# 128-row gathers and scatters in a new order of slots, a third matmul round in a branch of TensorE, and a 21st weight buffer

## The chip, the core and the metric

The kernel runs on one core of a Trainium2 chip. The metric is the device time of one execution in microseconds; a kernel's time is the median of its runs. The profile names the engines PE (TensorE, matmuls), PEld (its weight loads), DVE (VectorE), ACT (ScalarE), POOL (GpSimd) and SP (SyncE, which issues most DMAs); a "q" behind a name is the engine's sequencer or queue. The core's DMAs run on 16 DMA engines.

## What is computed

One decoder layer for 512 prompt tokens and 32 sample tokens (8 sequences of 4): a gated short convolution and a forgetting attention, merged by gates and projected, layer norm, and then a mixture of 16 experts, again with layer norm. The change lies in the experts:

```python
def hier_moe(x, w_group, w_router, w1, w3, w2):
    t = x.reshape(N * S, D)                       # 544 tokens (prompt and sample), D = 1024
    gp = jax.nn.softmax(t @ w_group)              # 4 groups, the best one is taken
    p_g, g_idx = lax.top_k(gp, 1)
    el_sel = ...                                  # the 4 experts of that group
    top_w, top_i = lax.top_k(jax.nn.softmax(el_sel), 2)
    gate = ...                                    # 544 x 16, two entries a row
    for e in range(16):
        h = jax.nn.silu(t @ w1[e]) * (t @ w3[e])  # 1024 -> 512
        y = y + gate[:, e:e + 1] * (h @ w2[e])    # 512 -> 1024
```

Each token goes to two of 16 experts, 68 tokens to an expert in the mean. All weights are float32; those of one expert are 6 MB.

## The kernel before

Up to about 447 us the kernel does the projections, the convolution, the attention, the output projection, the first layer norm and the routing. Then come the experts, which need 96 pieces of weights of 1 MB, and from about 720 us on the last sums and the second layer norm.

**Slots.** For each expert the tokens that chose it get positions 1, 2, 3 and so on (`pos`). `slot` (L370) holds the numbers 1 to `CAP` = 96. `onehots` compares both, `place` and `place_early` turn the result by a small matmul into 96 row numbers (`gix`), and `gate_of` puts the gates beside them. A slot without a token gets a row number past the end, and the DMA leaves such rows out. A branch at the end of the program (L1505) covers experts with over 96 tokens; with these inputs there are none.

**Gather and scatter.** `gather` (L1117) is an indexed DMA that POOL issues: it fetches the tokens' rows of 4 KB from `x1d` in DRAM into one of `NXG` = 3 buffers `xg`, a partition a slot. At the end of `down` (L1277) a second one adds the rows of `y` (one of `YB` = 2 buffers) to `acc` in DRAM. The last two experts (`KC` = 2) are not scattered but kept (`down_kept`) and summed on PE at the end.

**Matmuls of an expert.** `x_t` transposes the gathered rows. `up` multiplies in three rounds g = 0, 1, 2 of 32 slots each: the 32 slots are the stationary operand, and four matmuls, one for each quarter of the output columns, fill the array's four column strips. For each of 8 k-slices all three rounds run one after another. `glu` applies silu and the product, `h_t` transposes, and `down` works in rounds too: two for the first 64 slots, a third for slots 65 to 96. ACT scales `py` by the gates into `y`.

**The weights.** `raw_load` takes the buffers of a ring `RING` of 20 in turn and lets SP issue the load (L798). Pieces 13 and 14 wait for the last row of the first layer norm, pieces 17 to 21 (`GATED`) for the landing of the first gather, and from the 21st on each waits for the landing of the piece five before it (`AHEAD`, L800). A piece also waits until its buffer's last reader is done. The order is: the up pieces of expert e (four), then the down pieces of expert e-1 (two); at the end up pieces 0 and 1 of expert 15, the down pieces of 14, the rest of 15.

**The order in the loop** over experts, body e: first half of `up(e)`; transposes of x for e+1; second half of `up(e)`; `place` and `gather` for expert e+1+`NXG`; `down(e-1)`; `glu(e)`. Each engine runs its instructions in order; the framework adds the semaphores.

Of the kernel before, what the change touches and what calls it, by code (L numbers as in the profile page):

```python
# [55 lines left out]
WB = 4  # L56
KC = 2
ORDER = (4, 0, 1, 2, 3)
RING = ["pre"] * NPRE + ["rawb"] * NRB + ["raw"] * 2 + ["whl"] * 4 + ["half"] * 6
LAG = 2  # L60
MID = 4
FIRST = (1, 2, 3, 0, 4)
# [13 lines left out]
ZPE = (3, 4)  # L76
AHEAD = 5
THR0 = 20
YB = 2
NXG = 3  # L80
VW = 260
HELD = (13, 14)
GATED = (17, 18, 19, 20, 21)
# [4 lines left out]
def layer_kernel(ctx: ExitStack, tc: tile.TileContext, i_, o_):  # L88
# [238 lines left out]
    with tc.issue_after(ln_done.ins):  # L327
# [39 lines left out]
    nc.gpsimd.iota(prow, pattern=[[0, 1]], base=0, channel_multiplier=1)  # L367
    pcol = const.tile([128, 1], F32, name="pcol")
    nc.vector.tensor_copy(pcol, prow)
    slot = const.tile([128, CAP], BF, name="slot")  # L370
    nc.gpsimd.iota(slot, pattern=[[1, CAP]], base=1, channel_multiplier=0,
                   allow_small_or_imprecise_dtypes=True)
    rn = pa.tile([128, 2], F32, name="rn")
    rni = pa.tile([128, 2], I32, name="rni")
    nc.vector.tensor_single_scalar(rni[:, 0:1], prow, 5, op=ALU.arith_shift_right)
# [401 lines left out]
    def raw_load(e, j):  # L777
        shape, srcs = piece_of(e, j)
        shape = [128] + shape
        name = "wd" if j > 3 else "we"  # L780
        kind = ring_order[ring["n"] % len(ring_order)]
        ring["n"] += 1
        if kind == "half":
            r = half(name, shape)
        elif kind == "pre":
            r = pr_p.tile(shape, F32, name=name, tag="pre", bufs=NPRE)
        elif kind == "raw":
            r = base_p.tile(shape, F32, name=name, tag="raw", bufs=2)
        elif kind == "whl":
            r = base_p.tile(shape, F32, name=name, tag="whl", bufs=WB)  # L790
        else:
            r = p2.tile(shape, F32, name=name, tag="rawb", bufs=NRB)
        with ExitStack() as st:
            if ring["n"] in HELD:
                st.enter_context(tc.issue_after(last_x1.ins))
            elif ring["n"] > NPRE:
                st.enter_context(tc.issue_after(x_load.ins))
            lds = [nc.sync.dma_start(r if i is None else r[:, i], s) for s, i in srcs]  # L798
# [72 lines left out]
    xgs = []  # L871
    for b in range(NXG):
        xgs.append(p2.tile([128, D], F32, name=f"xg{b}"))
    nc.gpsimd.memset(xgs[0], 0.0)
    rsm = xgs[0]
    res = [rbig[t // 2][:, t % 2] for t in range(4)] + [rsm]
# [11 lines left out]
    for a in range(2):  # L888
        nc.gpsimd.tensor_mul(wr3[:, a, :, :NR], wrr,
                             gb[:, a].unsqueeze(2).to_broadcast([128, 8, NR]))  # L890
    ln_g, ln_b = lnw(1, xgs[1:])

    def small(name, shape, dt=F32):
        return p2.tile([128] + shape, dt, name=name)
# [45 lines left out]

    sums_last = []
    zt_last = {}
    wk = []

    def parts_of(x, n, cm=None):
        t = order[x]
# [2 lines left out]
        for k in range(4):  # L949
            nc.tensor.transpose(pp[:, k, :m], res[t][:m, (4 * n + k) * 128:(4 * n + k + 1) * 128], ident[:m, :m])  # L950
        if (x, n) == (NT - 1, 1):
            wk.append(ps_mm("wake")[:, 0])
# [34 lines left out]
    def ln1_out(x):  # L987
        t = order[x]
        m = rows_of(t)
        sc = mvs[:m, t]  # L990
        x1 = p2.tile([128, D], F32, name="x1", tag="y", bufs=YB) if x < NT - 1 else rsm
        if x < NT - 1:
            nc.scalar.activation(x1[:m], res[t][:m], AF.Identity, bias=sc[:, 4:5], scale=sc[:, 3:4])
            nc.vector.tensor_mul(x1[:m], x1[:m], ln_g[:m])
# [79 lines left out]
    flat = "p t e -> p (t e)"  # L1074
    asf = asb.rearrange("p t g e -> p t (g e)")
    mm(pps[:, :NT * NE], before, asf.rearrange(flat), start=False, stop=True, skip_group_check=True)
    keep_warm(wk[0], WK[3])
    pos = small("pos", [NT, NE], BF)
    nc.vector.scalar_tensor_tensor(pos.rearrange(flat), pps[:, :NT * NE], 1.0, asf.rearrange(flat),
# [7 lines left out]
    onehot = {}  # L1087

    def onehots(e):
        oh = p2.tile([128, NT, CAP], BF, name="soh", tag="soh", bufs=2)  # L1090
        nc.vector.tensor_tensor(oh, slot.unsqueeze(1).to_broadcast([128, NT, CAP]), bc(pos[:, :, e], CAP),
                                op=ALU.is_equal)
        onehot[e] = oh
        return oh

    def gate_of(e, parts):
        nc.vector.tensor_reduce(gat[:CAP, e:e + 1], parts, axis=AX, op=ALU.add)
        if e < E0:
            nc.scalar.activation(gat2[64:, e, 0:1], gat[:64, e:e + 1], AF.Copy)
            for q in range(4):  # L1100
                nc.scalar.activation(gat2[32 * q:32 * q + 32, e, 1:2], gat[64:96, e:e + 1], AF.Copy)

    def to_index(e, me):
        return nc.vector.tensor_scalar(gix[:CAP, e:e + 1], me, FAR, None, op0=ALU.add)  # L1104

    def place(e):
        pmt = ps_s("pmt")
        oh = onehots(e)
        for x in range(NT):
            mm(pmt[:CAP, :5], oh[:, x], mv[:, x, e], start=x == 0, stop=x == NT - 1)  # L1110
        me = p2.tile([CAP, 1], F32, name="me", tag="me", bufs=2)
        nc.vector.tensor_reduce(me, pmt[:CAP, 0:2], axis=AX, op=ALU.add)
        to_index(e, me)
        gate_of(e, pmt[:CAP, 2:5])

    def gather(e):
        return nc.gpsimd.indirect_dma_start(out=xgs[e % NXG][:CAP], out_offset=None, in_=x1d,  # L1117
                                     in_offset=bass.IndirectOffsetOnAxis(ap=gix[:CAP, e:e + 1], axis=0),
                                     bounds_check=T - 1, oob_is_err=False)

    def place_early(e):
        oh = onehots(e)
        pm0 = ps_s("pm0")
        for x in range(NT):
            mm(pm0[:CAP, :1], oh[:, x], tokh[:, x:x + 1], start=x == 0, stop=x == NT - 1)
        return to_index(e, pm0[:CAP, :1]), gather(e)

    def gates_early(e):
        oh = onehot[e]
        pg0 = ps_s("pg0")  # L1130
        for x in range(NT):
            mm(pg0[:CAP, :3], oh[:, x], mv[:, x, e, 2:5], start=x == 0, stop=x == NT - 1)
# [8 lines left out]
    oh1 = small("oh1", [NT, NE])  # L1141
    oh2 = small("oh2", [NT, NE])
# [54 lines left out]

    def rows_by_two(xr):  # L1200
        return xr.rearrange("c (j p r) -> c j r p", p=128, r=2)

# [21 lines left out]
    def up_round(g, pab, x, raws, ks):  # L1224
        out = pab.rearrange("p a b -> p (a b)")[:, 256 * g:256 * g + 256].rearrange("p (a b f) -> p a b f", a=2, f=32)
        for k in ks:
            rhs = raws[k // 2][:, :, k % 2].rearrange("p a (b c f) -> p a b c f", c=4, f=32)
            for c in range(4):
                mm(out[32 * c:32 * c + 32], x[:, k, 32 * g:32 * g + 32], rhs[:, :, :, c], start=k == 0 and g != 1,  # L1229
                   stop=k == 7, skip_group_check=True)  # L1230
# [25 lines left out]
    def down_round(r, py, h, raws, ks):  # L1256
        for k in ks:
            for q in range(4):
                g, c = (q % 2, 2 * (q // 2) + r) if r < 2 else (2, q)
                mm(py[32 * q:32 * q + 32, 256 * r:256 * r + 256], h[:, k, 32 * g:32 * g + 32],  # L1260
                   raws[k // 2][:, k % 2, 256 * c:256 * c + 256], start=k == 0 and r != 1, stop=k == 3,
                   skip_group_check=True)

    def down(e, h):
# [7 lines left out]
        nc.scalar.activation(y[:64, :512], py[:64, :512], AF.Copy, scale=gat[:64, e:e + 1])  # L1272
        nc.scalar.activation(y[:64, 512:], py[64:, :512], AF.Copy, scale=gat2[64:, e, 0:1])
        for q in range(4):
            nc.scalar.activation(y[64:, 256 * q:256 * q + 256], py[32 * q:32 * q + 32, 512:768], AF.Copy,  # L1275
                                 scale=gat2[32 * q:32 * q + 32, e, 1:2])
        nc.gpsimd.indirect_dma_start(out=acc, out_offset=bass.IndirectOffsetOnAxis(ap=gix[:CAP, e:e + 1], axis=0),  # L1277
                                     in_=y, in_offset=None, bounds_check=T - 1, oob_is_err=False,
                                     compute_op=ALU.add)

# [8 lines left out]
    def onehots_t(e):  # L1289
        if not ohT:  # L1290
            ohT["all"] = pr_p.tile([CAP, KC, NT, 128], F32R, name="ohT", tag="pre", bufs=NPRE)
        ohp = psum.tile([CAP, NT, 128], BF, name="ohp", tag="o", bufs=1)
        for x in range(NT):
            nc.tensor.transpose(ohp[:, x], onehot[e][:, x], identb)
        ohT[e] = ohT["all"][:, e - E0]
        nc.vector.tensor_copy(ohT[e], ohp)

# [7 lines left out]
    def down_kept(e, h):  # L1305
        yhl[e] = p2.tile([CAP, 2, D], F32R, name="yhl", tag="rawb", bufs=NRB)
        raws = down_raws(e)
        for n in range(2):
            py = ps_s("py")
            down_mm(py, raws, n, h)  # L1310
            keep_half(e, n, py[:CAP])

    nxt = x_t(0)
# [294 lines left out]
```

## Time and profile before

| | us |
|---|---|
| median of 3 runs (757.03 to 759.32) | 757.23 |
| the profiled execution | 758.94 |
| its span, first to last instruction | 757.2 |
| busy: PE / DVE / ACT / POOL | 725.2 / 354.3 / 246.0 / 114.7 |
| mean granted TensorE clock | 0.987 |
| bytes moved by DMA | 169.65 MB |

The profile is of one execution; its times are microseconds from the span's start. In a table by stretches of time, each row has the stretch, its length, the busy time of each engine with the count of instructions, the granted clock, the mean busy share of the 16 DMA engines, and the GB/s that they moved. A share can be a little above 1, since packets of an engine overlap. In the chain of work that ended last, each piece is the one that released the next; its columns are start, length, and what it was. A matmul call on float32 stands in the trace as two records.

### The profile page before, as it was taken

How to read it: one execution, taken by the hardware profiler on the slowest of the kernel's cores; microseconds unless marked ns; L12 is line 12 of the kernel's file. 1: busy time of each engine (PE TensorE's matmuls, PEld its weight loads, DVE VectorE, ACT ScalarE, POOL GpSimd, SP SyncE). 2: the span in 40 equal slices, each digit the busy share in tenths (PEclk: the TensorE clock that was granted, in tenths of full speed). 3: DMA queues.
4: the chain of work that ended last, by engine and by line, in shares of the span. 5: the costliest groups of instructions: out<-in, count | busy, mean ns of one | idle time of the engine just before them, and what ended most of it. 6: DMA issues, size and time to landing. Idle time of an engine off the chain costs nothing.

```text
span 757.2 us, 18645 instructions
## 1 busy us (share of the span) xinstructions
PE 725.2 (96%) x8102; PEld 563.8 (74%) x8102; DVE 354.3 (47%) x841; ACT 246.0 (32%) x502; POOL 114.7 (15%) x152
## 2 busy tenths in 40 slices
PE   7999999999999999999999998999999999898992
PEld 6899888898998999999975754656555565565551
DVE  3335667753435222333555684733454333441147
ACT  3443564533144222222423332322323322111234
POOL 5411000012441000000020521121111211100110
PEclk8999999999999999999999999999999999999997
DMA  9565302215552444434175589999999999999973
GB/s 226 188 219 173 108 29 82 70 50 194 168 168 85 144 131 147 168 112 167 57 277 182 203 327 341 339 370 337 358 371 334 363 360 338 343 375 376 386 177 121
DMA packets 65431, 169.65 MB, mean 224 GB/s; under 512 B 6144, under 2 KB 26672, under 8 KB 65344
## 3 DMA queue, kind: packets, MB, share of 16 engines
q1 hardware_dynamic: 55776, 141.08, 52.4%
q0 software_dynamic: 8992, 25.74, 12.8%
q8 instruction: 66, 1.08, 0.6%
q10 hardware_dynamic: 576, 1.57, 0.5%
q14 instruction: 21, 0.17, 0.1%
HBM read 157.40 MB, written 14.49 MB: 227 GB/s over the span
## 4 chain that ended last, share of the span: by engine, by line
PE 68%; DMA 26%; DVE 4%; issue 1%; SPq 0%; ACT 0%; DVEq 0%; ACTq 0%
DMA we<-in_w_dram 16%; PE pj L168 10%; PE pj L169 9%; PE pj L170 9%; DMA wd<-in_w_dram 8%; PE pab L1229 7%; PE py L170 2%; PE py L169 2%; PE py L168 2%; PE py L1260 2%; PE po L169 2%; PE po L170 2%; PE po L168 2%; PE py L1286 2%; PE S L566 1%; PE po L600 1%
## 5 line engine op out<-in xcount | busy, mean ns | idle before, releaser
L1229 PE MATMUL pab<-we,xgT 128*32 128x256 f32 x3072 | 172.3, 381 | 1.2 <-DMA we<-in_w_dram 1.0
L1229 PEld LDWEIGHTS pab<-we,xgT 128*32 128x32 f32 x3072 | 103.0, 111 | 65.3 <-issue 3.2
L1209 DVE STREAM_TRANSPOSE xgT<-xg 32x256 f32<-32x256 f32 x180 | 78.4, 435 | 117.1 <-PE pab L1229 106.4
L1260 PE MATMUL py<-wd,hT 128*32 128x256 f32 x1344 | 75.4, 380 | 4.5 <-DMA wd<-in_w_dram 2.9
L168 PE MATMUL pj<-xth,wgas 128*128 128x272 f32 x256 | 73.9, 289 | 0.0
L169 PE MATMUL pj<-xtl,wgas 128*128 128x272 f32 x256 | 73.9, 289 | 0.0
L170 PE MATMUL pj<-xth,wgas 128*128 128x272 f32 x256 | 73.6, 288 | 0.0
L1260 PEld LDWEIGHTS py<-wd,hT 128*32 128x32 f32 x1344 | 44.1, 110 | 30.7 <-ACT su L1242 3.8
L164 DVE TENSOR_TENSOR wgas<-wga,wgas 128x1024 fp32r<-128x1024 f32 x16 | 19.6, 1226 | 87.3 <-ACT wgas L163 87.3
L168 PEld LDWEIGHTS pj<-xth,wgas 128*128 128x128 f32 x256 | 48.3, 189 | 0.8 <-issue 0.8
L169 PEld LDWEIGHTS pj<-xtl,wgas 128*128 128x128 f32 x256 | 48.2, 188 | 0.0
L170 PEld LDWEIGHTS pj<-xth,wgas 128*128 128x128 f32 x256 | 48.2, 188 | 0.0
L1242 ACT ACTIVATE su<-pab 128x384 f32<-128x384 f32 x16 | 7.8, 490 | 104.8 <-PE pab L1229 104.8
L1277 POOL DMA_INDIRECT acc<-y,gix x14 | 20.1, 1439 | 129.0 <-ACT y L1275 129.0
L168 PE MATMUL pj<-xth,wqks 128*128 128x272 f32 x128 | 38.6, 302 | 0.0
L169 PE MATMUL pj<-xtl,wqks 128*128 128x272 f32 x128 | 36.9, 289 | 0.0
L170 PE MATMUL pj<-xth,wqks 128*128 128x272 f32 x128 | 36.9, 289 | 0.0
L163 ACT ACTIVATE wgas<-wga 128x1024 fp32r<-128x1024 f32 x16 | 16.9, 1055 | 47.4 <-DMA wga<-in_w_in_dram 46.5
L1117 POOL DMA_INDIRECT xg<-x1d,gix x16 | 15.7, 980 | 101.9 <-DVE gix L1104 76.5
L1272 ACT ACTIVATE y<-py,gat 64x512 f32<-64x512 f32 x14 | 9.5, 682 | 64.5 <-PE py L1260 36.1
L840 ACT ACTIVATE sg<-pj 128x544 f32<-128x544 f32 x16 | 9.9, 617 | 54.4 <-PE pj L170 53.8
L169 PE MATMUL po<-wos,mxh 128*128 128x512 f32 x64 | 26.0, 406 | 0.9 <-DVE wos L164 0.9
(426 smaller groups left out, 1560.8 us busy)
## 6 DMA issues: line engine op xcount, KB each, us to landing
we<-in_w_dram SPq DMA_DIRECT2D x128, 512.0 KB, 14.0
wd<-in_w_dram SPq DMA_DIRECT2D x32, 1024.0 KB, 16.0
wga<-in_w_in_dram SPq DMA_DIRECT2D x8, 1024.0 KB, 6.7
wqk<-in_w_in_dram SPq DMA_DIRECT2D x4, 1024.0 KB
wo<-in_w_o_dram SPq DMA_DIRECT2D x4, 1024.0 KB, 5.0
xa<-in_x_prompt_dram SPq DMA_DIRECT2D x4, 512.0 KB, 11.8
ckb<-cdr POOLq DMA_DIRECT2D x8, 256.0 KB, 3.7
wcg<-in_w_in_dram SPq DMA_DIRECT2D x2, 1024.0 KB
```

The costliest lines, as they stand in the source:

```text
L163: nc.scalar.activation(h, src, AF.Copy)
L164: (eng or nc.vector).tensor_sub(l, src, h.bitcast(F32))
L168: mm(out, al, bh, start=first, stop=False)
L169: mm(out, ah, bl, start=False, stop=False)
L170: return mm(out, ah, bh, start=False, stop=last)
L840: nc.scalar.activation(h2(e), pm, AF.Sigmoid)
L1117: return nc.gpsimd.indirect_dma_start(out=xgs[e % NXG][:CAP], out_offset=None, in_=x1d, in_offset=bass.IndirectOffsetOnAxis(ap=gix[:CAP, e ...
L1209: nc.vector.transpose(x[32 * j:32 * j + 32, :, 32 * g:32 * g + 32].rearrange("p (j r) s -> p j r s", r=2), rows[32 * g:32 * g + 32, :, :, ...
L1229: mm(out[32 * c:32 * c + 32], x[:, k, 32 * g:32 * g + 32], rhs[:, :, :, c], start=k == 0 and g != 1, stop=k == 7, skip_group_check=True)
L1260: mm(py[32 * q:32 * q + 32, 256 * r:256 * r + 256], h[:, k, 32 * g:32 * g + 32], raws[k // 2][:, k % 2, 256 * c:256 * c + 256], start=k == ...
L1277: nc.gpsimd.indirect_dma_start(out=acc, out_offset=bass.IndirectOffsetOnAxis(ap=gix[:CAP, e:e + 1], axis=0), in_=y, in_offset=None, bounds ...
L1286: pe_last.append(mm(py[:CAP], h[:, k], raws[k // 2][:, k % 2, n * 512:(n + 1) * 512], start=k == 0, stop=k == 3))
```

## The change

- **Slots.** `slot` has 128 columns in four blocks of 32: slots 1 to 32, 65 to 96, 33 to 64, and a last block of -1 that nothing matches. One-hots, row numbers, gathers, `y` and scatters have 128 rows. Rows without a token keep a row number past the end. The round of slots 65 to 96 is now round 1 of `up` and round 2 of `down`.
- **Third round in a branch.** A matmul counts the tokens of each expert (`full`), VectorE packs "more than 64" into one bit an expert, and PE alone loads the number into a register. In `up` and `down` of the first 14 experts the round of slots 65 to 96 stands in a branch on its expert's bit, three branches an expert, 16 matmul calls in each. It runs at the end of each half of `up`, and at the end of `down`, no longer interleaved with the other rounds; in the last two experts it is moved likewise, without a branch. As a skipped round leaves its columns unwritten, two PSUM banks are taken once, their columns set to zero by ACT, and used in turn for `up` and `down`.
- **Buffers.** `NXG` is 2 and `YB` is 1. The freed 8 KB a partition are the ring's 21st weight buffer (`ext`); before the experts it holds gain and offset of the first layer norm.
- **ACT.** The gated copies into `y` are four of 32x512 and four of 32x256, instead of two of 64x512 and four of 32x256; the copies of the gates grow from five to six.

```diff
-RING = ["pre"] * NPRE + ["rawb"] * NRB + ["raw"] * 2 + ["whl"] * 4 + ["half"] * 6
+RING = ["pre"] * NPRE + ["rawb"] * NRB + ["raw"] * 2 + ["whl"] * 4 + ["half"] * 6 + ["ext"]
...
-YB = 2
-NXG = 3
+YB = 1
+NXG = 2
...
-    slot = const.tile([128, CAP], BF, name="slot")
-    nc.gpsimd.iota(slot, pattern=[[1, CAP]], base=1, channel_multiplier=0,
-                   allow_small_or_imprecise_dtypes=True)
+    slot = const.tile([128, 128], BF, name="slot")
+    for b, first_slot in enumerate((1, 65, 33)):
+        nc.gpsimd.iota(slot[:, 32 * b:32 * b + 32], pattern=[[1, 32]], base=first_slot, channel_multiplier=0,
+                       allow_small_or_imprecise_dtypes=True)
+    nc.gpsimd.memset(slot[:, 96:], -1.0)
...
+        elif kind == "ext":
+            r = p2.tile(shape, F32, name=name, tag="ext", bufs=1)
...
+    lw1 = p2.tile([128, 2, D], F32, name="lw1", tag="ext", bufs=1)
...
-    ln_g, ln_b = lnw(1, xgs[1:])
+    ln_g, ln_b = lnw(1, (lw1[:, 0], lw1[:, 1]))
...
-        x1 = p2.tile([128, D], F32, name="x1", tag="y", bufs=YB) if x < NT - 1 else rsm
+        x1 = xgs[0] if x == NT - 1 else xgs[1] if x % 2 else p2.tile([128, D], F32, name="x1", tag="y", bufs=YB)
...
+    full = ps_s("full")
+    for x in range(NT):
+        mm(full[:, :NE], onesb, asf[:, x], start=x == 0, stop=x == NT - 1)
...
     def gather(e):
-        return nc.gpsimd.indirect_dma_start(out=xgs[e % NXG][:CAP], out_offset=None, in_=x1d,
-                                     in_offset=bass.IndirectOffsetOnAxis(ap=gix[:CAP, e:e + 1], axis=0),
+        return nc.gpsimd.indirect_dma_start(out=xgs[e % NXG], out_offset=None, in_=x1d,
+                                     in_offset=bass.IndirectOffsetOnAxis(ap=gix[:, e:e + 1], axis=0),
                                      bounds_check=T - 1, oob_is_err=False)
...
+    bits = p2.tile([1, NE], F32, name="bits")
+    many = p2.tile([1, 2], F32, name="many")
+    manyi = p2.tile([1, 1], I32, name="manyi")
+    for e in range(NE):
+        nc.gpsimd.memset(bits[:, e:e + 1], float(2 ** e))
+    nc.vector.scalar_tensor_tensor(bits, full[:1, :NE], 64.0, bits, op0=ALU.is_gt, op1=ALU.mult,
+                                   accum_out=many[:, 0:1])
+    nc.vector.tensor_copy(manyi, many[:, 0:1])
+    third_of = nc.values_load(manyi[:1, 0:1], engines=[mybir.EngineType.PE], min_val=0, max_val=2 ** NE - 1)
...
+    def third(e):
+
+        return tc.If((third_of >> e) & 1 > 0) if e < E0 else ExitStack()
+
+    def bank():
+        turn.append(0)
+        return banks[len(turn) % 2]
+
     def up(e, a, pab, x):
-        for j in (2 * a, 2 * a + 1):
-            raws = {j: raw_e(e, j)}
-            for k in (2 * j, 2 * j + 1):
-                for g in range(3):
-                    up_round(g, pab, x, raws, (k,))
+        raws = {}
+        ks = range(4 * a, 4 * a + 4)
+        for k in ks:
+            if k % 2 == 0:
+                raws[k // 2] = raw_e(e, k // 2)
+            for g in (0, 2):
+                up_round(g, pab, x, raws, (k,))
+        with third(e):
+            up_round(1, pab, x, raws, ks)
...
     def down(e, h):
-        y = p2.tile([CAP, D], F32, name="y", tag="y", bufs=YB)
-        py = ps_mm("py").rearrange("p a b -> p (a b)")
+        y = ys[e % YB]
+        py = bank().rearrange("p a b -> p (a b)")
+        raws = {}
         for j in range(2):
-            raws = {j: raw_e(e, 4 + j)}
+            raws[j] = raw_e(e, 4 + j)
             for k in (2 * j, 2 * j + 1):
-                for r in range(3):
+                for r in range(2):
                     down_round(r, py, h, raws, (k,))
-        nc.scalar.activation(y[:64, :512], py[:64, :512], AF.Copy, scale=gat[:64, e:e + 1])
-        nc.scalar.activation(y[:64, 512:], py[64:, :512], AF.Copy, scale=gat2[64:, e, 0:1])
+        with third(e):
+            down_round(2, py, h, raws, range(4))
+        for b in (0, 64):
+            nc.scalar.activation(y[b:b + 32, :512], py[b:b + 32, :512], AF.Copy, scale=gat[b:b + 32, e:e + 1])
+            nc.scalar.activation(y[b:b + 32, 512:], py[b + 32:b + 64, :512], AF.Copy, scale=gat2[b + 32:b + 64, e, 0:1])
...
-        nc.gpsimd.indirect_dma_start(out=acc, out_offset=bass.IndirectOffsetOnAxis(ap=gix[:CAP, e:e + 1], axis=0),
+        nc.gpsimd.indirect_dma_start(out=acc, out_offset=bass.IndirectOffsetOnAxis(ap=gix[:, e:e + 1], axis=0),
...
+    banks.append(ps_mm("moe"))
+    for b in banks:
+        nc.scalar.activation(b.rearrange("p a b -> p (a b)")[:, 256:768].rearrange("p (a b) -> p a b", a=4),
+                             ident.unsqueeze(1).to_broadcast([128, 4, 128]), AF.Copy, scale=0.0)
...
-        pab = ps_mm("pab")
+        pab = bank()
```

More of the change, by code (lines that the diff above doesn't have):

```diff
@@ L942, in layer_kernel @@
     zt_last = {}
-    wk = []
+    wk, banks, turn = [], [], []
     def parts_of(x, n, cm=None):
@@ L951, in parts_of @@
         if (x, n) == (NT - 1, 1):
-            wk.append(ps_mm("wake")[:, 0])
+            banks.append(ps_mm("moe"))
+            wk.append(banks[0][:, 0])
             keep_warm(wk[0], WK[0])
@@ L1089, in onehots @@
     def onehots(e):
-        oh = p2.tile([128, NT, CAP], BF, name="soh", tag="soh", bufs=2)
-        nc.vector.tensor_tensor(oh, slot.unsqueeze(1).to_broadcast([128, NT, CAP]), bc(pos[:, :, e], CAP),
+        oh = p2.tile([128, NT, 128], BF, name="soh", tag="soh", bufs=2)
+        nc.vector.tensor_tensor(oh, slot.unsqueeze(1).to_broadcast([128, NT, 128]), bc(pos[:, :, e], 128),
                                 op=ALU.is_equal)
@@ L1098, in gate_of @@
         if e < E0:
-            nc.scalar.activation(gat2[64:, e, 0:1], gat[:64, e:e + 1], AF.Copy)
+            for b in (0, 64):
+                nc.scalar.activation(gat2[b + 32:b + 64, e, 0:1], gat[b:b + 32, e:e + 1], AF.Copy)
             for q in range(4):
-                nc.scalar.activation(gat2[32 * q:32 * q + 32, e, 1:2], gat[64:96, e:e + 1], AF.Copy)
+                nc.scalar.activation(gat2[32 * q:32 * q + 32, e, 1:2], gat[32:64, e:e + 1], AF.Copy)
     def to_index(e, me):
-        return nc.vector.tensor_scalar(gix[:CAP, e:e + 1], me, FAR, None, op0=ALU.add)
+        return nc.vector.tensor_scalar(gix[:, e:e + 1], me, FAR, None, op0=ALU.add)
     def place(e):
@@ L1109, in place @@
         for x in range(NT):
-            mm(pmt[:CAP, :5], oh[:, x], mv[:, x, e], start=x == 0, stop=x == NT - 1)
-        me = p2.tile([CAP, 1], F32, name="me", tag="me", bufs=2)
-        nc.vector.tensor_reduce(me, pmt[:CAP, 0:2], axis=AX, op=ALU.add)
+            mm(pmt[:, :5], oh[:, x], mv[:, x, e], start=x == 0, stop=x == NT - 1)
+        me = p2.tile([128, 1], F32, name="me", tag="me", bufs=2)
+        nc.vector.tensor_reduce(me, pmt[:, 0:2], axis=AX, op=ALU.add)
         to_index(e, me)
@@ L1124, in place_early @@
         for x in range(NT):
-            mm(pm0[:CAP, :1], oh[:, x], tokh[:, x:x + 1], start=x == 0, stop=x == NT - 1)
-        return to_index(e, pm0[:CAP, :1]), gather(e)
+            mm(pm0[:, :1], oh[:, x], tokh[:, x:x + 1], start=x == 0, stop=x == NT - 1)
+        return to_index(e, pm0[:, :1]), gather(e)
     def gates_early(e):
@@ L1131, in gates_early @@
         for x in range(NT):
-            mm(pg0[:CAP, :3], oh[:, x], mv[:, x, e, 2:5], start=x == 0, stop=x == NT - 1)
+            mm(pg0[:CAP, :3], oh[:, x, :CAP], mv[:, x, e, 2:5], start=x == 0, stop=x == NT - 1)
         gate_of(e, pg0[:CAP, :3])
@@ L1137, in layer_kernel @@
     keep_warm(wk[0], WK[4])
+    bits = p2.tile([1, NE], F32, name="bits")
[7 more added lines that the diff above has]
+    third_of = nc.values_load(manyi[:1, 0:1], engines=[mybir.EngineType.PE], min_val=0, max_val=2 ** NE - 1)
     gl = lgt[:, :, :NG]
     el = lgt[:, :, NG:]
-    oh1 = small("oh1", [NT, NE])
-    oh2 = small("oh2", [NT, NE])
+    picks = p2.tile([128, 2, NT, NE], F32, name="picks", tag="su", bufs=1)
+    oh1, oh2 = picks[:, 0], picks[:, 1]
     nc.vector.scalar_tensor_tensor(oh1, rank[:, :, NG:], 0.0, asf, op0=ALU.is_equal, op1=ALU.mult)
@@ L1258, in down_round @@
             for q in range(4):
-                g, c = (q % 2, 2 * (q // 2) + r) if r < 2 else (2, q)
+                g, c = (q // 2 * 2, 2 * (q % 2) + r) if r < 2 else (1, q)
                 mm(py[32 * q:32 * q + 32, 256 * r:256 * r + 256], h[:, k, 32 * g:32 * g + 32],
@@ L1262, in down_round @@
                    skip_group_check=True)
+    ys = [p2.tile([128, D], F32, name="y", tag="y", bufs=YB) for _ in range(YB)]
+    for y in ys:
+        nc.gpsimd.memset(y[96:], 0.0)
     def down(e, h):
-        y = p2.tile([CAP, D], F32, name="y", tag="y", bufs=YB)
-        py = ps_mm("py").rearrange("p a b -> p (a b)")
+        y = ys[e % YB]
+        py = bank().rearrange("p a b -> p (a b)")
+        raws = {}
         for j in range(2):
-            raws = {j: raw_e(e, 4 + j)}
+            raws[j] = raw_e(e, 4 + j)
             for k in (2 * j, 2 * j + 1):
-                for r in range(3):
+                for r in range(2):
                     down_round(r, py, h, raws, (k,))
-        nc.scalar.activation(y[:64, :512], py[:64, :512], AF.Copy, scale=gat[:64, e:e + 1])
-        nc.scalar.activation(y[:64, 512:], py[64:, :512], AF.Copy, scale=gat2[64:, e, 0:1])
+        with third(e):
+            down_round(2, py, h, raws, range(4))
+        for b in (0, 64):
+            nc.scalar.activation(y[b:b + 32, :512], py[b:b + 32, :512], AF.Copy, scale=gat[b:b + 32, e:e + 1])
+            nc.scalar.activation(y[b:b + 32, 512:], py[b + 32:b + 64, :512], AF.Copy, scale=gat2[b + 32:b + 64, e, 0:1])
         for q in range(4):
-            nc.scalar.activation(y[64:, 256 * q:256 * q + 256], py[32 * q:32 * q + 32, 512:768], AF.Copy,
+            nc.scalar.activation(y[32:64, 256 * q:256 * q + 256], py[32 * q:32 * q + 32, 512:768], AF.Copy,
                                  scale=gat2[32 * q:32 * q + 32, e, 1:2])
-        nc.gpsimd.indirect_dma_start(out=acc, out_offset=bass.IndirectOffsetOnAxis(ap=gix[:CAP, e:e + 1], axis=0),
+        nc.gpsimd.indirect_dma_start(out=acc, out_offset=bass.IndirectOffsetOnAxis(ap=gix[:, e:e + 1], axis=0),
                                      in_=y, in_offset=None, bounds_check=T - 1, oob_is_err=False,
@@ L1293, in onehots_t @@
         for x in range(NT):
-            nc.tensor.transpose(ohp[:, x], onehot[e][:, x], identb)
+            nc.tensor.transpose(ohp[:, x], onehot[e][:, x, :CAP], identb)
         ohT[e] = ohT["all"][:, e - E0]
@@ L1311, in down_kept @@
             keep_half(e, n, py[:CAP])
+    banks.append(ps_mm("moe"))
+    for b in banks:
+        nc.scalar.activation(b.rearrange("p a b -> p (a b)")[:, 256:768].rearrange("p (a b) -> p a b", a=4),
+                             ident.unsqueeze(1).to_broadcast([128, 4, 128]), AF.Copy, scale=0.0)
     nxt = x_t(0)
```

## The prediction

> **What bounds the kernel now.** First the page's head and its chain of work that ended last, then the table by stretches of time, the queue's own waits, and the DMA view of the expert stage.
>
> ```profile
> span 757.2 us, 18645 instructions
> ...
> PE 68%; DMA 26%; DVE 4%; issue 1%; SPq 0%; ACT 0%; DVEq 0%; ACTq 0%
> ```
>
> ```profile
> core 0: us, PE busy (x) PEld busy (x) DVE busy (x) ACT busy (x) POOL busy (x), PEclk, DMA share, GB/s
> 460.00:492.00 32.00, 32.00 (x566) 18.70 (x562) 21.72 (x58) 10.20 (x38) 3.82 (x4) 0.99 1.03 364
> 476.00:636.00 160.00, 160.00 (x2939) 95.74 (x2931) 77.12 (x197) 47.15 (x120) 23.79 (x20) 1.00 1.02 354
> 636.00:652.00 16.00, 15.85 (x293) 9.29 (x289) 6.50 (x17) 3.71 (x7) 2.41 (x2) 1.00 0.94 312
> 652.00:700.00 48.00, 42.46 (x768) 28.53 (x764) 13.27 (x29) 7.92 (x15) 4.26 (x3) 1.00 1.02 377
> 452.00:710.00 258.00, 248.18 (x4418) 150.93 (x4417) 108.71 (x282) 68.20 (x172) 35.42 (x30) 0.99 1.01 356
> ```
>
> All that the change touches lies after 447 us. There PE is busy without a gap until 636, and the DMA engines are busy without a gap too. Which of the two is the bound is read from their pace.
>
> ```profile
> we<-in_w_dram SPq DMA_DIRECT2D x72, 512.0 KB, 14.9
> wd<-in_w_dram SPq DMA_DIRECT2D x21, 1024.0 KB, 16.3
> ```
>
> ```profile
> 472.43 10.50 PE pab L1229 x192
> 482.93 0.32 PE pmt L1110 x5
> 483.25 5.32 PE py L1260 x96
> ...
> 525.68 16.22 DMA wd<-in_w_dram
> ...
> 709.68 5.39 PE py L1286 x12
> ```
>
> The first fence is the DMA view of 525 to 710 us: 72 halves and 21 whole pieces are 57 pieces of 1 MB in 185 us, 3.25 us each, so the six pieces of an expert take 19.5 us. The second is the chain: it gives PE 10.50 + 0.32 + 5.32 = 16.1 us for the same expert. PE is faster than its supply and lives on the 16 pieces (2.7 experts) that the code lets load before the first gather lands; the stock is gone near 650, where PE drops to 42.46 of 48 us and the chain, from 525 on nearly all "DMA we" and "DMA wd", ends at the piece that PE needs at 709.68. From there to the end 47.5 us of PE and VectorE work follow. **The bound is the stream of weight pieces.** What holds the stream back?
>
> ```profile
> SPq L798 <- DMA we<-in_w_dram: 87.1, 46, 4.2
> SPq L798 <- DMA wd<-in_w_dram: 51.6, 19, 3.9
> ...
> SPq L798 <- PE pab L1229: 0.8, 3, 0.4
> ```
>
> In the queue's waits of 525 to 710 us, SP waits 138.7 us for the landing of a piece five before (the bounded queue, L800) and 0.8 us for PE's up projections to free a buffer. So neither a faster PE nor one more buffer moves the stream; only less or better spread work on the DMA engines does.
>
> **The change part by part.** The sum is made against the profiled execution: 758.94 us, of which 757.2 are span. It lies 1.7 us above the median of the runs shown, 757.23; the difference that I work out is taken off that median.
>
> *Third round in a branch.* The reference's router, on the given inputs, sends 63, 58, 79, 72, 54, 64, 63, 69, 67, 57, 64, 58, 82, 84, 69 and 85 tokens to the experts. Of the 14 that can skip, eight have at most 64. A third of 10.50 + 5.32 is 5.3 us, times eight 42 us of PE, and with the 5.7 us that PE idles between 636 and 700 (48 - 42.46, 16 - 15.85) a reserve of some 48 us. All of it lies under the stream: counted 0. What branches cost comes out of this reserve; their price is the second rival.
>
> *Gathers and scatters.* This is where the stream can gain.
>
> ```profile
> q0 software_dynamic: 2304, 5.60, 14.5%
> ...
> xg<-x1d,gix POOLq DMA_INDIRECT x11, 7.7
> ```
>
> ```profile
> DMA  6778999899999999999996998799599967955578
> ```
>
> The first fence is the DMA view of 476 to 636 us: the indexed rows take 14.5% of 16 engines x 160 us = 371 us for 5.60 MB, which is 1367 rows of 4 KB, 0.27 us a row. The second is the busy share of the 16 engines in 40 slices of 639 to 644 us. It falls to 5 to 7 tenths, about ten or eleven engines of 16, just where the table above has its 0.94 and 312 GB/s. I read this as 96 rows dealt six by six in order of slot: with 66 filled slots 11 engines work and five run ahead until the bounded queue stops them. After 457 us there are 28 such transfers: 28 x 6 = 168 rows, 46 us, on the engine with most.
>
> How 128 rows are dealt, no row here shows. Ends: if each engine gets four of the slots 1 to 64, an engine without further ones has 112 rows, 15 us less; the one that also gets four of each expert above 64 (14 of the 28 transfers, two of them with three) has 166, 0.5 us less. If eight neighbours go to one engine, eight engines have 224 rows, 15 us more. Which engine paces the stream is not shown either. The nearest row is the share: 1.03 with all engines fed (460 to 492) against 1.01 in the mean says that 2%, or 258 x 0.02 = 5 us, are lost to idle engines. I take **-5 us**. [...]
>
> Second, stretching. With gathers beside the stream 354 GB/s move, without them (652 to 700, scatters only) 377, at the same share 1.02. These bytes include the gathers' own, so packets are slower by 6%: 160 x 0.06 = 9.8 us. If that comes from six-row dealing crossing the weights' own paths it goes, if from gathering as such it stays: ends 0 and -9.8, and with no row between them I take half, **-4.9 us**.
>
> *What POOL and SBUF give for it.*
>
> ```profile
> L400 POOL DMA_INDIRECT pages<-in_cache_k_dram,pgi x16: 942/950/1327, 24.8 to 198.6; - x16
> L1117 POOL DMA_INDIRECT xg<-x1d,gix x16: 952/981/1047, 450.7 to 643.9; - x16
> L1277 POOL DMA_INDIRECT acc<-y,gix x14: 1403/1434/1546, 492.3 to 706.1; - x14
> L1275 ACT ACTIVATE y<-py,gat x56: 462/465/468, 490.0 to 705.4; 32x256 f32<-32x256 f32 x56
> L1272 ACT ACTIVATE y<-py,gat x14: 682/682/683, 488.6 to 702.5; 64x512 f32<-64x512 f32 x14
> ...
> DMA to landing us min/median/max: 8.2/8.4/8.6
> ```
>
> A 128-row gather is issued in 0.95 us (L400), a 96-row one in 0.98: issue does not grow, 0. ACT fills y with four copies of 0.68 and four of 0.465, 4.6 us instead of 3.2. With one y buffer the cycle is 4.6 + 1.4 + 8.4 = 14.4 us, inside the 19.5 us of an expert; only where PE runs ahead on skipped experts (10.9 us) do ACT's copies, and the activation queued behind them, wait some 4 us, at PE's expense: 0 while the reserve lasts. Gather e+3 is issued after expert e+1 has been read and used two experts later, at least 21 us for a landing of 7.7: 0. The 21st buffer takes effect on the 21st piece, at about 461 us; by the queue's waits above it is worth 0. The clears of two banks, 16 memsets and PE's wait for the register lie between 450 and 457 us; queued behind that wait are only the keep-warm matmuls and the transposes that wait for the first gather anyway: 0. With 21 buffers the last pieces lie in other ones: the kept result of expert 14 takes a buffer of its own down weights, so its write waits for the end of that projection (709.68 + 5.39). Its reader comes after the up projection that follows: 0.
>
> *What is late at both ends.*
>
> ```profile
> L1091 DVE TENSOR_TENSOR soh<-slot,pos x16: 645/658/660, 448.5 to 617.0; 128x480 bf16<-128x480 bf16 x16
> 449.29 0.35 PE L1125 MATMUL pm<-tokh,soh 128*96 128x1 f16 x5
> ...
> 450.65 6.27 DMA xg<-x1d,gix
> ```
>
> The one-hot that leads to the first gather grows from 0.658 by a third, 0.2 us; five counting matmuls like the five of L1125 (0.35 us) stand before it on PE, most of it on the path. The gathered rows hold back pieces 17 to 21, so the stream starts later: **+0.5 us**. In the last expert the second half of the up projection now runs its third round after both pieces: when the last piece is late, 32 matmul calls follow it instead of 24, 8 x 10.50/96 = **+0.9 us** (96 calls to the 192 records of an expert).
>
> Sum: -5.0 - 4.9 + 0.5 + 0.9 = -8.5 us, 750.4 for the profiled execution, **748.7** as a median. With each term at its ends the forecast's own range is 737 to 755.
>
> **The rivals.**
>
> *Eight rows to an engine.* The slots 1 to 32 and 33 to 64 then fall on eight engines with 224 rows each, and the pacing engine gains 56 rows. For it: the plateau shows dealing by neighbours today. Against: nothing in the trace. Between the 15 us of the price and nothing (if engines idle today become the full ones) I take 10: 767 us. It decides from the point where any engine has over 168 rows.
>
> *Branches on PE.*
>
> ```profile
> L1505 PEldq COMPARE_BRANCH  x1: 3737/3737/3737, 740.7 to 740.7; - x1
> L1505 DVEq COMPARE_BRANCH  x1: 76/76/76, 752.1 to 752.1; - x1
> ```
>
> The only branch that PE takes today, over the far body at the end, holds its sequencer 3.74 us; VectorE's takes 0.08. The new ones are 42, of which 24 jump over 16 calls. At 0.08 they cost 3 us of the reserve, at 3.74 90 us: 42 over the reserve, 799 us. PE becomes the bound from 48/24 = 2.0 us a jump. Against it: the jumps are short, where the one measured is over the largest body of the program. [...]
>
> *Nothing moves.* The engine that paces today keeps 166 of 168 rows and the stretching stays: -0.5 + 0.5 to 0.9, 757 to 758 us. For it: the stream's bytes and bounded queue are unchanged. [...]
>
> **How the numbers follow.** Forecast 0.63, nothing moves 0.15, eight rows 0.15, branches 0.07. A measurement of this kernel tells about 0.3% (2.3 us) from no change. Faster is the forecast but for its upper edge, 0.62; same 0.15 with that edge, 0.16; slower the rest, 0.22. The range reaches from the forecast's low end, 737, over nothing to 768 for eight rows; outside are the branches and some edges, under 2 in 10.
>
> **What would show it.** Right: PE idle in every skipped expert from about 520 us on, the chain on "DMA we" and "DMA wd" as now, more than 360 GB/s in the gather stage, no plateau at 5 to 7 tenths, last pieces some 10 us earlier, the first gather at 451. Wrong: plateaus at eight of 16 engines with under 350 GB/s (eight rows); PE branches of 2 us or more with the chain on PE (branches); 354 GB/s again (nothing moves). I would be wrong above all if the paced engine is not among those that lose rows.

## The result: 751.1 us, by other steps than forecast

The changed kernel takes 751.13 us (749.87 to 751.76, 4 runs), the kernel before 757.62 beside it: 0.9909 of it, with a 95% interval of 0.9888 to 0.993. The forecast was 748.7. The profiled execution took 751.76 us, 7.2 less than the 758.94 before. The sum is nearly the forecast one, but two of its parts are not: the stream of weights gained twice as much as predicted, and the end gave most of the excess back.

First the table by stretches of time of the changed kernel, to be held against the rows in the prediction; the columns are the same.

```profile
476.00:636.00 160.00, 146.29 (x2513) 92.27 (x2509) 86.32 (x213) 65.31 (x154) 28.70 (x22) 0.98 1.03 390
636.00:652.00 16.00, 15.68 (x292) 11.15 (x288) 6.36 (x14) 6.76 (x13) 1.59 (x1) 1.00 1.03 391
652.00:700.00 48.00, 45.74 (x723) 26.41 (x717) 9.71 (x19) 12.47 (x23) 5.51 (x5) 1.00 0.98 365
```

The gather stage moves 390 GB/s where it moved 354, and the stretch at 636 with 312 GB/s is gone. But the share of busy engines in 476 to 636 rose only from 1.02 to 1.03. So little of the gain is idle engines put to work; the rest is that the same busy time moves more. The DMA view of that stretch says for whom, first before the change, then after.

```profile
q1 hardware_dynamic: 13664, 50.68, 86.0%
q0 software_dynamic: 2304, 5.60, 14.5%
```

```profile
q1 hardware_dynamic: 15134, 56.13, 87.9%
q0 software_dynamic: 3159, 5.91, 13.9%
```

The columns are packets, MB, and the share of 16 engines x 160 us = 2560 us. For the weights (q1) that is 0.860 x 2560 / 50.68 = 43.4 us of engine time per MB before and 40.1 after; for the indexed rows (q0) 0.27 us a row before and 0.139 x 2560 / (5.91 MB / 4 KB) = 0.25 after. The weights, whose loads the change doesn't touch, got 8% cheaper.

How early that made the weights shows where PE starts on the down projection of expert 14. From PE's timeline, before and after:

```profile
707.55 1.96 PE L1286 MATMUL py<-wd,hT 128*96 128x512 f32 x4
...
723.88 5.31 PE L1286 MATMUL py<-wd,hT 128*96 128x512 f32 x12
```

```profile
687.97 7.11 PE L1328 MATMUL py<-wd,hT 128*96 128x512 f32 x16
...
709.47 3.73 PE L1328 MATMUL py<-wd,hT 128*96 128x512 f32 x4 [5.82 <-DMA wd<-in_w_dram]
715.81 6.53 PE L1328 MATMUL py<-wd,hT 128*96 128x512 f32 x8 [2.62 <-DMA wd<-in_w_dram]
```

Expert 14 starts 19.6 us sooner (the first rows), but from there to the end of the span it is 750.0 - 687.97 = 62.0 us, where it was 757.2 - 707.55 = 49.65. The last expert's down projection (723.88 before, 709.47 after) now waits for its own pieces, 5.82 and 2.62 us. SyncE's timeline shows why. Before:

```profile
704.63 2.90 SPq L798 DMA_DIRECT2D wd<-in_w_dram  x2
707.63 3.87 SPq L1363 DMA_DIRECT2D z<-x1d  x3
714.35 2.56 SPq L1370 DMA_DIRECT2D z<-acc  x2
```

After, and the chain of work that ended last:

```profile
682.53 4.13 SPq L1410 DMA_DIRECT2D z<-x1d  x3
696.55 0.81 SPq L1417 DMA_DIRECT2D z<-acc  x2
697.42 2.14 SPq L803 DMA_DIRECT2D wd<-in_w_dram  x2
```

```profile
462.72 9.04 DMA we<-in_w_dram
...
678.68 8.79 DMA we<-in_w_dram
687.47 9.03 DMA acc<-y,gix
697.42 1.63 SPq L803
699.10 16.67 DMA wd<-in_w_dram
715.81 6.53 PE py L1328 x8
```

Before, the last two weight pieces stood ahead of the loads of z, the sums' other operand. Now they stand behind them, and the loads of `acc` wait for the last scatter (687.47 to 696.5 in the chain). In the queue's own waits of 525 to 710 us this is one row:

```profile
SPq L1417 <- DMA acc<-y,gix: 9.8, 1, 9.8
```

The order goes with the branches. In the kernel 'nobr' below, which lacks only the branches and so computes every third round, the two weight pieces stand in front again, as its rows there show. The likely way is by the scheduler, which puts the instructions of a block in order, where each branch ends a block: before, the loop over experts was one block, and the last down loads were moved up in it; after, they stand in the last block, where the program names the z loads first. That is inferred from the orders seen, not shown.

### The profile page after: what moved, and what is told of

The parts are those of the page before. It is cut to its first block, busy times and chain, and to the rows that moved or that the text cites. A ratio compares the mean times of both kernels' runs of the same rounds, so it can differ in the third digit from the quotient of the medians.

```text
span 750.0 us, 17347 instructions
## 1 busy us (share of the span) xinstructions
PE 695.7 (93%) x7339; PEld 546.3 (73%) x7339; DVE 359.9 (48%) x844; ACT 269.0 (36%) x546; POOL 119.7 (16%) x172
## 3 DMA queue, kind: packets, MB, share of 16 engines
HBM read 159.49 MB, written 16.32 MB: 234 GB/s over the span
## 4 chain that ended last, share of the span: by engine, by line
PE 55%; DMA 36%; DVE 4%; SPq 2%; issue 1%; POOL 1%; ACT 0%; DVEq 0%; ACTq 0%; POOLq 0%
DMA we<-in_w_dram 23%; PE pj L168 10%; PE pj L169 10%; PE pj L170 10%; DMA wd<-in_w_dram 8%; PE py L170 2%; PE py L169 2%; PE py L168 2%; PE S L569 2%; PE po L603 1%; PE po L169 1%; PE po L170 1%; PE po L168 1%; SPq L803 1%; PE ptp L592 1%; DMA acc<-y,gix 1%
## 5 line engine op out<-in xcount | busy, mean ns | idle before, releaser
L1251 PE MATMUL moe<-we,xgT 128*32 128x256 f32 x2560 | 147.7, 381 | 8.3 <-DMA we<-in_w_dram 3.4
L1251 PEld LDWEIGHTS moe<-we,xgT 128*32 128x32 f32 x2560 | 93.3, 110 | 59.1 <-issue 14.6
L1294 PE MATMUL moe<-wd,hT 128*32 128x256 f32 x1088 | 67.1, 395 | 5.5 <-PEq L1270 2.5
L164 DVE TENSOR_TENSOR wgas<-wga,wgas 128x1024 fp32r<-128x1024 f32 x16 | 19.6, 1226 | 87.0 <-ACT wgas L163 87.0
L1294 PEld LDWEIGHTS moe<-wd,hT 128*32 128x32 f32 x1088 | 38.8, 113 | 30.0 <-issue 8.9
L1314 ACT ACTIVATE y<-moe,gat 32x512 f32<-32x512 f32 x28 | 19.0, 679 | 60.6 <-DMA acc<-y,gix 27.2
L1319 POOL DMA_INDIRECT acc<-y,gix x14 | 22.6, 1616 | 102.0 <-ACT y L1317 85.8
L1276 ACT ACTIVATE su<-moe 128x384 f32<-128x384 f32 x16 | 7.9, 491 | 69.3 <-PE moe L1251 43.0
L1328 PE MATMUL py<-wd,hT 128*96 128x512 f32 x32 | 19.2, 756 | 8.4 <-DMA wd<-in_w_dram 8.4
## 6 DMA issues: line engine op xcount, KB each, us to landing
wqk<-in_w_in_dram SPq DMA_DIRECT2D x4, 1024.0 KB, 10.1
```

The source lines that it names most:

```text
L164: (eng or nc.vector).tensor_sub(l, src, h.bitcast(F32))
L1314: nc.scalar.activation(y[b:b + 32, :512], py[b:b + 32, :512], AF.Copy, scale=gat[b:b + 32, e:e + 1])
L1328: pe_last.append(mm(py[:CAP], h[:, k], raws[k // 2][:, k % 2, n * 512:(n + 1) * 512], start=k == 0, stop=k == 3))
```

## The experiments

All times are medians; "ratio" is to the kernel before on the same chip, with its 95% interval. Unless a chip is named, the kernel before took 757.0 to 757.7 us there.

### The order of the last loads

**early**: the changed kernel, with the last two pieces named ahead of the z loads.

```diff
+    last_wd = down_raws(NE - 1)
     for x in range(3):
         z_bank(x)
     for x in range(NT):
         z_load(x)
...
-    raws = down_raws(e)
+    raws = last_wd
```

> The changed kernel, with SyncE's loads of expert 15's two down pieces issued ahead of the five z loads (in the changed kernel they stand behind them, so that they wait for the last scatter). Theory A (the stream won some 21 us, 709.68 to 688.86 at expert 14's last down piece, and 13.6 us of it are given back by this order): the end comes 10 to 13 us sooner than in the changed kernel, a profiled span of 737 to 740 us; PE's wait of 8.4 us for these pieces falls under 1 us. Theory B (the end hangs on the scatter of expert 13 and the z loads behind it, whatever the order): the z loads land some 5 us later instead, and the span stays at 746 to 750 us.

738.33 us, ratio 0.9754 (0.9736 to 0.9772), profiled span 735.2: theory A, with a span a little below its 737 to 740. PE's timeline:

```profile
686.76 7.11 PE L1328 MATMUL py<-wd,hT 128*96 128x512 f32 x16
701.46 1.02 PE L1328 MATMUL py<-wd,hT 128*96 128x512 f32 x2
702.79 4.45 PE L1328 MATMUL py<-wd,hT 128*96 128x512 f32 x10
```

There is no wait for weights any more, and from expert 14 to the end it is 735.2 - 686.76 = 48.4 us. In these two executions the order costs the changed kernel 62.0 - 48.4 = 13.6 us. The z loads from `x1d` do come later, as theory B had it (issued from 685.61 us on, 682.53 in the changed kernel; POOL waits 15.2 us for one, there 10.1), but the waits of 684 to 735 us show that VectorE, their reader, waits for them only once:

```profile
DVE z L1474 <- DMA z<-acc: 1.3, 1, 1.3
```

**zadd**: the last pieces between the z loads from `x1d` and those from `acc`, so behind the bytes but not behind the wait.

```diff
     for x in range(NT):
         z_load(x)
+    last_wd = down_raws(NE - 1)
...
-    raws = down_raws(e)
+    raws = last_wd
```

> The changed kernel with expert 15's two down pieces issued between the three z loads from x1d and the two from acc, so they stand behind 1.5 MB of z loads as in the changed kernel but no longer behind SyncE's wait of 9.8 us for the last scatter. Theory N (that wait is what held the pieces back): they are issued by about 691 us in place of 699 and land by about 706, 737 to 743 us. Theory O (the bytes of the z loads ahead of them are what held them back): 746 to 751 us, as the changed kernel (751.1 us).

751.47 us, but on a chip where the kernel before took 766.01: ratio 0.9811 (0.9791 to 0.9832). Against 0.991 and 0.975 neither theory fits alone. So the three orders ran again on one chip (before: 759.31).

> The changed kernel itself, beside the two other orders of SyncE's last loads on one chip, since 'zadd' ran where the kernel before took 766 us and not 757. From the ratio on record, 0.991 of the kernel before; 62 us from PE's start on expert 14's down projection to the end.

> As 'zadd'. If SyncE's wait for the scatter is some 8.5 of the 13.6 us and the z loads' bytes the other 5 (53.5 us from PE's start on expert 14's down projection to the end in 'zadd', 62.0 in the changed kernel, 48.4 in 'early'): 7 to 10 us faster than the changed kernel and 4 to 6 slower than 'early'. If the wait is all of it: within 2 us of 'early'.

> As 'early': 12 to 14 us faster than the changed kernel beside it, 0.975 of the kernel before.

750.90, 743.48 and 741.58 us (early_b: 737.75 to 743.75); ratios 0.9908 (0.9875 to 0.9941), 0.9798 (0.9766 to 0.983), 0.9774 (0.9726 to 0.9821). zadd_b is 7.4 us faster than the changed kernel, as expected, but only 1.9 slower than early_b, where 4 to 6 was expected. And early_b is 9.3 us faster than the changed kernel, where 12 to 14 was expected; its four runs spread by 6 us, so these medians tell the price of the order no better than 9 to 14 us. Its profiled execution also starts on expert 14 later, at 689.92 against 687.77 us in after_b. Counted from that start, the profiled executions leave the stream out. PE's timeline of zadd_b, span 742.4:

```profile
686.92 7.11 PE L1328 MATMUL py<-wd,hT 128*96 128x512 f32 x16
704.22 3.67 PE L1328 MATMUL py<-wd,hT 128*96 128x512 f32 x8 [0.79 <-DMA wd<-in_w_dram]
711.04 5.35 PE L1328 MATMUL py<-wd,hT 128*96 128x512 f32 x8 [3.14 <-DMA wd<-in_w_dram]
```

From expert 14 to the end it is 55.5 us (53.5 in zadd), between 48.4 (early, and early_b too) and 61 to 62 (after_b and the changed kernel). Of some 13 us, the wait for the scatter is 6 to 8.5, the bytes of the z loads in front 5 to 7. Both are the order. These figures hold the slow matmuls behind PE's waits too, of which the last section tells: of the 2 us between zadd and zadd_b, 1.7 are the last eight matmuls (3.67 and 5.35 us).

### Which part made the stream faster

**rows96e**: as early, with 96 rows in gathers and scatters; the new slot order, the branch and the 21st buffer stay.

```diff
-        return nc.gpsimd.indirect_dma_start(out=xgs[e % NXG], ...
+        return nc.gpsimd.indirect_dma_start(out=xgs[e % NXG][:CAP], ...
...
-  ... gix[:, e:e + 1] ..., in_=y
+  ... gix[:CAP, e:e + 1] ..., in_=y[:CAP]
```

> As 'early', but gathers and scatters take 96 rows again (slots in the new order, branch and 21 buffers kept). Theory A (the dealing of 128 rows alone made the stream faster): 350 to 360 GB/s in the gather stage, expert 14's last down piece lands at 707 to 712 us, the time is 754 to 760 us. Theory C (the 21st buffer or the skipped rounds made the stream faster): over 380 GB/s, time within 2 us of 'early'.

760.94 us, ratio 1.0048 (1.0031 to 1.0066). The table by stretches:

```profile
476.00:636.00 160.00, 141.20 (x2385) 88.29 (x2377) 79.81 (x199) 62.76 (x150) 25.50 (x21) 0.97 1.01 352
```

352 GB/s, as before the change: theory A, though the time is 0.9 us above its range. The weights cost 43.3 us of engine time per MB again (85.0% of 2560 us for 50.25 MB in the DMA view of this stretch). Without the 128 rows the rest of the change costs 4 us rather than winning any. The 0.9 us of the later start are among them; what the others are was not separated.

**scat96**: as early, gathers of 128 rows, scatters of 96.

> As 'early', gathers of 128 rows, but scatters of 96. Theory I (the weights' packets are slowed by gathers of 96 rows, whose packets went from 159 to 275 ns before to 159 ns after, while scatters' packets took 327 ns in both): 739 to 744 us, over 380 GB/s in 476 to 636. Theory J (each of the two kinds of transfer does its share): half of the 22 us between 'rows96e' and 'early', 747 to 752 us, 365 to 375 GB/s.

744.43 us, ratio 0.9818 (0.9798 to 0.9838), and

```profile
476.00:636.00 160.00, 145.51 (x2529) 91.70 (x2521) 85.95 (x213) 64.25 (x153) 26.27 (x22) 1.00 1.02 383
```

The time lies just above theory I, and the weights cost 40.5 us per MB (86.9% for 54.92 MB). Of the 22.6 us between rows96e and early, the gathers bring 16.5, the scatters 6.1. The runs are of two chips; by the ratios it is 17.4 and 4.8.

**plain128**: as early, but slots 1 to 96 in plain order on the 128 partitions, and the third round, gates and copies of y as in the kernel before.

```diff
-    for b, first_slot in enumerate((1, 65, 33)):
+    for b, first_slot in enumerate((1, 33, 65)):
...
-            for g in (0, 2):
+            for g in (0, 1):
...
-            up_round(1, pab, x, raws, ks)
+            up_round(2, pab, x, raws, ks)
```

> As 'early' (738.3 us), with 128-row gathers and scatters, branch and 21 buffers, but the slots lie on the partitions in their plain order 1 to 96, and the third round, the gates and the copies of y follow that order. [...] Theory H (it is the count of 128 rows alone that speeds up the stream, the order of slots is for nothing): within 2 us of 'early'.

759.92 us, ratio 1.0019 (1.0006 to 1.0032). The table by stretches, and the DMA view of 476 to 636:

```profile
476.00:636.00 160.00, 137.36 (x2369) 82.87 (x2361) 79.80 (x199) 47.13 (x120) 27.53 (x21) 0.98 0.98 355
```

```profile
q1 hardware_dynamic: 13673, 50.71, 83.9%
q0 software_dynamic: 3068, 5.73, 13.4%
```

Rows for rows the same transfers, and all of the gain is gone: theory H falls. In none of the 40 slices of the DMA view are the engines under 8 tenths busy, so there is no plateau, but the mean share is 0.98 against 1.03 after the change, 5% less. As much is lost another way: the weights cost 0.839 x 2560 / 50.71 = 42.4 us of engine time per MB (40.1 after the change), while a row costs 0.25 us as after the change. So the order of slots costs twice, in idle engines and in slower packets of the weights, and the second was not in the price of the prediction's rival.

No row shows which engine moved which rows. The order of slots changes the partitions that the filled rows lie on, and by that it may change the engines that move them: that an uneven load of the engines, and not something on the side of the partitions, slows the weights is the author's reading of 42.4 against 40.1 us per MB, and not shown.

### Skipped rounds, branches and buffers

**nobr**: the changed kernel without branches.

```diff
-        return tc.If((third_of >> e) & 1 > 0) if e < E0 else ExitStack()
+        return ExitStack()
```

> The changed kernel with the third round computed for every expert (no branch; without the blocks of the branches the scheduler puts the last down pieces ahead of the z loads by itself). Theory D (a faster stream makes PE the bound: PE's work without its 5.7 us of idle time would end expert 14 at 704 us, 15 us behind the landing of its weights): 749 to 753 us, PE busy without a gap to 700 us, 370 to 378 GB/s over 476 to 636 as SyncE now waits for PE to free buffers. Theory E (PE's reserve still covers the third rounds, as the prediction had it): the time of 'early', 737 to 742 us.

751.57 us, ratio 0.9924 (0.9902 to 0.9946): theory D. The table by stretches, and PE's timeline:

```profile
476.00:636.00 160.00, 160.00 (x2957) 95.13 (x2950) 79.65 (x198) 61.79 (x152) 25.64 (x20) 1.00 1.03 393
```

```profile
701.37 7.11 PE L1328 MATMUL py<-wd,hT 128*96 128x512 f32 x16
```

SyncE's timeline has the last weight pieces ahead of the z loads:

```profile
682.08 2.93 SPq L803 DMA_DIRECT2D wd<-in_w_dram  x2
691.14 6.08 SPq L1410 DMA_DIRECT2D z<-x1d  x3
```

PE has no idle time and starts on expert 14's down projection at 701.37, 14.6 us later than in early, although the stream is as fast. (The 370 to 378 GB/s that theory D added were wrong; it stays at 393, since SyncE still waits for landings, 121 us of 525 to 700.) With all third rounds PE is the bound, and the kernel gains about what PE had idled before: 5.4 us, for the 5.7 between 636 and 700.

**taken**: as early, but the threshold is -1, so all 42 branches are there and nothing is skipped.

> As 'early', but the branch's threshold lets every expert run its third round, so all 42 branches are there and none skips work. PE is the bound then, as in 'nobr' (751.6 us), so that the branches' own price shows. [...] Theory L (each costs PE about 3 us, as the few long ones in the changed kernel do): 42 x 3 = 126 us more, 860 us or more.

751.47 us, ratio 0.9915 (0.9897 to 0.9934), the same as without branches (751.57): theory L falls. The records of the branches, of the up projections in taken, then of both projections in the changed kernel:

```profile
L1270 PEldq COMPARE_BRANCH  x56: 67/130/327, 464.5 to 674.5; - x56
```

```profile
L1270 PEldq COMPARE_BRANCH  x40: 68/176/3115, 463.6 to 657.4; - x40
...
L1311 PEldq COMPARE_BRANCH  x20: 68/196/3164, 481.0 to 680.9; - x20
```

A branch that falls through leaves two records (28 branches, 56 records), of 0.13 us in the median, and as 42 such branches cost no time, they are hidden behind running matmuls: from 476 to 636 us PE is busy for 159.49 of 160 us in taken, for 160.00 in nobr. In the changed kernel a branch that skips its round leaves one record; the median over both kinds is 0.18 to 0.20 us, and three of the 24 skipping branches take 3.06 to 3.16 us (the longest of each line is its row's maximum), the others under 0.4. Together the three are 9 us of PE time that the stream covers. Why these three are long and the others not, no run shows.

**noexte** and **y2**: early with 20 weight buffers, and that with two y buffers in the tile freed.

```diff
-RING = ... + ["half"] * 6 + ["ext"]
+RING = ... + ["half"] * 6
```

```diff
-    ys = [p2.tile([128, D], F32, name="y", tag="y", bufs=YB) for _ in range(YB)]
+    ys = [lw1[:, 0], lw1[:, 1]]
...
-        y = ys[e % YB]
+        y = ys[e % 2]
```

> As 'early', but with 20 weight buffers instead of 21 (the 21st tile holds only the two layer-norm rows of the stage before). Theory A (the buffer is worth nothing as SyncE waits for landings, not for buffers): within 1.5 us of 'early'. Theory F (the 21st buffer is what keeps the queue fed): 3 to 8 us slower than 'early'.

> As 'noexte' (738.0 us), with two y buffers in place of one: the two lie in the 8 KB tile that holds the layer-norm rows of the stage before, which is the 21st weight buffer in the changed kernel. Theory A (ACT's waits for the scatter, 15 to 27 us in all, come out of PE's reserve): within 1.5 us of 'noexte'. Theory M (they end up on the path): 3 to 8 us faster than 'noexte'.

738.03 us, ratio 0.9743 (0.9727 to 0.9759), and 738.01 us, ratio 0.9739 (0.9716 to 0.9762): both as early. The 21st buffer is worth nothing here, and ACT's waits for the single y buffer (17.9 us in noexte, none in y2) cost nothing:

```profile
ACT y L1314 <- DMA acc<-y,gix: 17.9, 4, 5.0
```

So the best kernel of this study is early, or noexte, which is as fast with a buffer less: 2.5% below the kernel before.

## Why the prediction was right, and where its steps were not

In terms of the profiled executions, by its own steps:

| step | forecast, us | measured, us |
|---|---|---|
| rows: balance and stretching | -5.0 and -4.9 | -20.5 together (about -3 and -18) |
| later start | +0.5 | +0.9 |
| third round behind the last piece | +0.9 | +0.9, hidden here |
| from expert 14's down pieces to the end | 0 | +12.4 |
| sum | -8.5 | -7.2 |

The measured column is -19.6 for PE's start on expert 14, of which the start takes +0.9, and 62.0 - 49.65 = 12.4 from there on.

**What bounds the kernel: right.** The chain of the changed kernel from 462.72 to 687 is one DMA of weights after another, and SyncE still waits for landings of weights, 67.3 and 45.7 us of 525 to 710. What follows from it, that faster PE and one more buffer don't move the stream, is shown by rows96e (352 GB/s, 354 before) and noexte (738.03 us, early 738.33).

**Balance and stretching: both there, the size of stretching far too small.** The DMA view from 460 us to the landing of expert 14's last down piece (709.68 before, 688.86 after) tells the two apart, since nearly the same bytes move in both:

```profile
q1 hardware_dynamic: 21971, 81.56, 87.6%
q0 software_dynamic: 3025, 7.45, 12.7%
```

```profile
q1 hardware_dynamic: 21955, 81.46, 89.2%
q0 software_dynamic: 3888, 7.45, 12.4%
```

The stretch falls from 249.68 to 228.86 us, by 20.8. The packets of the weights take 0.876 x 249.68 = 218.7 us of all 16 engines before and 0.892 x 228.86 = 204.1 after, 14.6 less; the indexed rows take 31.7 and 28.4, 3.3 less. These 18 us are stretching, for 4.9 forecast. The other 3 are the higher share of busy engines, balance, for 5 forecast. So the term that was mis-sized is stretching, and it was cut twice. The prediction took it from the stages with and without gathers (354 against 377 GB/s) and halved that, because no row told dealing from gathering. But 377 was no upper end: scatters of 96 rows ran in that stretch too, and scat96 shows that they stretch as well (383 GB/s in the gather stage, 390 after the change). The forecast also counted only the 160 us of the gather stage. How rows are dealt to the engines, from which the prediction made the ends of its balance term, no run shows; what the runs show in its place is the share of busy engines and the time per MB.

**The end: wrong.** "From there to the end 47.5 us of PE and VectorE work follow" was taken over unchanged. The step that failed is the one that priced the branches only as instructions on PE. With them the order of SyncE's last loads changed as well, and the last two weight pieces came to stand behind the z loads and the scatter. Right for the kernel with the old order, where early has 48.4 for before's 49.65, it was 12.4 us short for this one. The two errors, -10.6 us on the rows and +12.4 at the end, nearly cancel; the closeness of the sum is chance. Nor does the forecast's own range of 737 to 755 follow from its terms: their ends (-15 and -0.5, -9.8 and 0, with +1.4 for the late start and the third round) give 734 to 758.

**Third round, counted 0: right alone, not in the sum.** The prediction has the 42 us as cover and nothing more. With the stream 20 us faster the cover is spent: early against nobr makes the skipped rounds worth 13 us. In the changed kernel this is just what its order of loads takes back, so that it is no faster than nobr.

**Later start and last third round: about right.** The chain after has the first gather at

```profile
451.49 6.36 DMA xg<-x1d,gix
```

and so ends it 0.9 us later, for 0.5 forecast. The third round's 0.9 us show in the chain of noexte, where 64 records (32 calls) follow the last piece:

```profile
681.10 15.61 DMA we<-in_w_dram
...
696.84 3.66 PE moe L1251 x64
```

48 would take 2.7 us. In the changed kernel PE then waits for the down pieces anyway.

**The rivals.** Whether any engine gets eight rows of a transfer, no run shows. Slots in plain order, in plain128, cost 1.4 us against the kernel before by the ratio, where the rival had 10 more, and 21.6 us against the new order, in early. Branches of 3.7 us each did not come; the long ones are three of 42. "Nothing moves" is refuted by the 390 GB/s, 354 before.

## What to carry to other kernels

When an indexed transfer runs beside the stream that bounds a kernel, try the count and the order of its rows, and price them in the other stream's time per MB (here 42.4 us in plain order, 40.1 in the new one) as well as in the share of busy engines (0.98 and 1.03). Here branches on PE changed the order of SyncE's last loads, with the last weights issued at 697.42 us, behind the z loads, and at 682.08, ahead of them, in nobr: after adding a branch, compare the order of every queue near the end with the order before. And a saving that is hidden under the bound is worth counting again with the bound moved by the gain that you forecast.

## What the hardware showed that was not expected

PE's wait near the end costs more than its length. The table by stretches for the changed kernel, and then for early:

```profile
700.00:711.00 11.00, 5.10 (x22) 2.41 (x15) 1.84 (x3) 1.98 (x3) 3.02 (x4) 0.86 0.98 295
711.00:716.00 5.00, 2.38 (x4) 0.47 (x3) 0.00 (x0) 0.00 (x0) 0.00 (x0) 0.50 0.99 201
716.00:724.00 8.00, 8.00 (x15) 3.02 (x16) 1.90 (x4) 0.68 (x1) 0.00 (x0) 0.65 0.04 8
```

```profile
700.00:711.00 11.00, 10.39 (x31) 4.79 (x30) 4.08 (x9) 2.62 (x4) 3.20 (x4) 1.00 0.69 166
```

With PE's two waits of 5.8 and 2.6 us the granted clock falls: it is 0.50 from 711 to 716 us, and 0.65 over the next 8 us; in early, without a wait for weights, it stays at 1.00. Eight matmuls of the last down projection then take 6.53 us. At the pace of the twelve at 723.88 before the change (5.31 us) they would take 3.5. So some 3 of the 13.6 us are the slow clock after the wait, not the wait. In after_b the same eight take 5.37 us, so there it is nearer to 2. What sets the clock no run shows; that it falls by the waits is read from the changed kernel and early side by side.
